# Two dense layers and a mixture of experts on one core: one gather for two pairs of experts, 21 weight slots, and activations placed at the weights' address modulo 256

## The chip, the core and the metric

The kernel runs on one core of a Trainium2 chip. The metric is the device time of one execution in microseconds (us), the median of several runs. The core's engines work side by side, each through its own queue in order: PE (TensorE, matrix products; PEld is its loading of the stationary operand, which the profile lists apart), DVE (VectorE), ACT (ScalarE), POOL (GpSimd) and SP (SyncE, which issues nearly all DMA transfers here). [...] The matrices come from HBM by DMA.

## The reference

The input is 256 rows of 1024 numbers in fp32. Two ordinary layers (a mixer, a gated feed-forward part and a gated per-layer embedding each) are followed by a convolution block, and that by a mixture of 32 experts, of which each row takes two:

```python
def hier_moe(h, w_rg, b_rg, w_re, b_re, w_gate, w_up, w_down):
    ...
    gate = grp_p[:, None] * jax.nn.softmax(top_val, axis=-1)
    expert = grp[:, None] * MOE_EXPERTS_PER_GROUP + top_idx
    ...
    def run_block(args):
        xb, e = args
        hid = jax.nn.silu(xb @ w_gate[e]) * (xb @ w_up[e])
        return hid @ w_down[e]
...
x = x + g1 * y
h = rmsnorm_2(x, norm_ffn_g[i]) * (1 + sc2) + sh2
x = x + g2 * hier_moe(h, ...)
return rmsnorm_2(x, final_g)
```

An expert has three matrices: gate and up of 1024 x 512, down of 512 x 1024, all fp32.

## The kernel before

**Dense part (0 to about 787 us).** Rows are two halves `h` of 128. Every fp32 product is made of three products of fp32r addends: an activation and a weight are each split into a high and a low addend, and `mm3` (L109) adds high x high, high x low and low x high in PSUM through `mm` (L101), the one place where these products are issued. The stationary operand is a block of 128 x 128 activations (`xTh`/`xTl`; in places `yTh`/`yTl`, `aTh`/`aTl`, `kvh`, `qlh`, `pTh` and their low parts), the moving one 512 columns of weights in a tile `hl` (high addends in its first half, low ones in its second; split by ACT and DVE in `prep`, L146). In the convolution's input product the roles are swapped for five of its eight parts: `hl` is stationary and `xTh`/`xTl` move, 256 columns.

**Where the operands lie.** A tile's address within its partition follows from the order and the sizes in which the pools hand them out. Of the built program, modulo 256 bytes: every `hl` starts at 224. `xTh`, `xTl` and the second layer's `aTh`, `aTl` start at 160; `yTh`, `yTl`, the first layer's `aTh`, `aTl`, and `kvh`, `qlh` with their low parts start at 128. Steps within these tiles are multiples of 512 bytes, so each product has one of these residues. Of products with 512 columns there are 2,112 with the stationary operand at 160 and 408 at 128; with 256 to 384 columns there are 276 more, and 240 with the roles swapped (stationary at 224, moving at 160).

**Experts (about 798 us to the end).** The 32 experts run as 16 pairs. For pair `i`:
- `pair_slots(i, False)` builds on DVE a table of 256 rows x 128 slots (64 per expert) that has a row's norm factor `rstd` where the row goes to the slot; `pair_slots(i, True)` the same with the gate's weight.
- `gather` (L1541) multiplies the rows `X` by this table on PE, in fp32: 2 PSUM banks, in each 4 blocks of 128 columns x 2 halves. ACT and DVE then bring the blocks to `xg`, in turn, with gain and shift. An fp32 product is two passes on PE, so a gather is 32 rows of the trace.
- `expert` (L1570): blocks `b` = 0, 1 (gate) and 2, 3 (up), each with one weight slot of each expert: 8 products of 64 x 512 that run side by side two by two.
- `down` (L1592): first `before(0)`, then the transposed hidden state, `before(1)`, and blocks 4 and 5 with the down matrices. The results, split in two addends, are added into the output by `combine2` during the next pair (L1633, L1634).

`back(j)` hangs the other work on these points: at j = 0 the combine for one half of the rows and the gather of pair i + 1, at j = 1 the other half and `way_back`. For pair 0 the gather stands in front of the expert (first bank) and after block 0 (second bank, `start`).

**Weights of the experts.** `preload` (L1106) has SP issue 192 transfers of 1 MB (numbered q; pair i uses q = 12 i to 12 i + 11, block b two of them) into 24 slots used in turn: 3 `early`, 2 `nexts`, 3 `ring`, 5 `wring`, 8 `split`, and 3 more: two tiles `w` and `spare`, which takes the place of `xTh` when the dense part has ended. A transfer into a slot waits for PE's last product with what is in it, and SP's queue is in order.

Of the kernel before, what the change touches and what calls it, by code (L numbers as in the profile page):

```python
# [8 lines left out]
F32 = mybir.dt.float32  # L9
# [19 lines left out]


@with_exitstack
def kernel(ctx, tc, A, out, stop=None):
# [4 lines left out]

    RING, SPLIT, EARLY, NEXT, WRING, MORE = SLOT_PLAN
    SLOTS = RING + SPLIT + EARLY + NEXT + WRING + MORE
    const = ctx.enter_context(tc.tile_pool(name="const", bufs=1))  # L40
# [530 lines left out]
    def ffn_ple(l, end, mid=None):  # L571
# [534 lines left out]
    def preload(n):  # L1106
        while len(moe_w) < min(n, 6 * NEXP):
# [3 lines left out]
            if s_ < EARLY:  # L1111
                t_ = early.tile([128, 2048], F32, name="ew", tag="ew")
            elif s_ < EARLY + NEXT:
                t_ = nexts.tile([128, 2048], F32, name="nw", tag="nw")
            elif s_ < EARLY + NEXT + RING:
                t_ = ring.tile([128, 2048], F32, name="raw", tag="raw")
            elif s_ < EARLY + NEXT + RING + WRING:
                t_ = wring.tile([128, 2048], F32, name="wr", tag="wr")
            elif s_ < SLOTS - MORE:
                t_ = split.tile([128, 2048], F32, name="hl", tag="hl")  # L1120
            else:
                t_ = spare if s_ == SLOTS - 1 else moe.tile([128, 2048], F32, name="w", tag="w", bufs=MORE - 1)
            pieces = 2 if q == 6 * NEXP - 1 else 1
# [361 lines left out]
    late = []  # L1485
    G1, G2, G3 = TG["rt"]
    for n in range(2):
        def ev_co(h, pt, n=n):
            t_ = small.tile([128, 512], F32, name="xf", tag="xf")
            tt(t_, pt, g1row[:, n * 512:(n + 1) * 512], MUL)  # L1490
            resid(h, n, t_)
            if n == 1 and h == 0:
                norm_stat(h)
                fill(G1, lambda: r_transpose(0, 0))
                fill(2, lambda: r_transpose(0, 1))
                fill(G2, lambda: r_logits(0))
                fill(G3, lambda: late.append(r_choose(0)))
# [34 lines left out]

    spare = xp.tile([128, 2048], F32, name="spare", tag="xTh")
    preload(SLOTS)

    yhl = xp.tile([128, 2, D], F32R, name="yhl", tag="xTl")
    yh, yl = yhl[:, 0, :], yhl[:, 1, :]
    xg = moe.tile([128, 8, 128], F32, name="xg")


    def gather(oh_r, n, gs=(0, 1)):  # L1541

        for g in gs:
            tp = pbank("w").rearrange("p (k t) -> p k t", k=4)
            for i in range(4):
                k = 4 * g + i
                for h in range(2):
                    T.matmul(tp[:, i, :n], X[:, h, k * 128:(k + 1) * 128], oh_r[:, h, :n], start=h == 0, stop=h == 1)  # L1548
            for i in range(4):
                k = 4 * g + i  # L1550
                if i % 2:
                    ts(xg[:, k, :n], tp[:, i, :n], moe_g[:, k:k + 1], modc[:, 24 + k:25 + k], MUL, ADD)
                else:
                    act(xg[:, k, :n], tp[:, i, :n], AF.Identity, scale=moe_g[:, k:k + 1], bias=modc[:, 24 + k:25 + k])
    def way_back(oh_g, n, exact=False, into=None):
# [13 lines left out]

    def expert(weights, n_e, between=None, after0=None):  # L1570

        n = 64 * n_e
        pg, pu = pbank("gu"), pbank("gu")
        for b in range(4):
            ws = weights(b)
            o = pg if b < 2 else pu
            for kk in range(4):
                for e in range(n_e):
                    k = 4 * (b % 2) + kk
                    T.matmul(o[64 * e:64 * e + 64, :], xg[:, k, 64 * e:64 * e + 64],  # L1580
                             ws[e][:, kk * 512:(kk + 1) * 512], start=k == 0, stop=k == 7)
# [56 lines left out]

    def pair_slots(i, back):
        t_ = moe.tile([128, 2, 128], F32, name="oh", tag="oh_g" if back else "oh_r", bufs=1)  # L1640
        for h in range(2):
            for e in range(2):
                q = 2 * i + e
                sc = gate[:, h, q:q + 1] if back else rstd[h][:, 0:1]
                ts(t_[:, h, 64 * e:64 * e + 64], iota64, rank[:, h, q:q + 1], sc, EQ, MUL)
        onehots[i, back] = t_

# [6 lines left out]
    def start_ends():  # L1654
# [3 lines left out]
        G.dma_start(rows_[0:1, D:2 * D], A["final_g"])  # L1658
        end.extend([rows_[:, 0:D], rows_[:, D:2 * D], R, early.tile([128, 2048], F32, name="ew", tag="ew")[:, 0:D]])

# [15 lines left out]

    prev = None
    pair_slots(0, False)
    gather(onehots[0, False], 128, (0,))

# [5 lines left out]
    def start():  # L1686
        gather(onehots[0, False], 128, (1,))
        for f in late:
            f()
        pair_slots(0, True)  # L1690
        ts(more, cnt, 64.0, None, ALU.is_gt)
# [4 lines left out]
        V.tensor_copy(nblk, upto[0:1, 31:32])  # L1696
        pair_slots(1, False)

    for i in range(NP):
# [7 lines left out]
        def back(j, i=i, prev=prev, final=final):  # L1707
            if prev is not None and j < 2:
                combine2(j, prev[0], i == 1, final)
                if final:  # L1710
                    gather_up(j)
            if not final and j == 0:
                gather(onehots[i + 1, False], 128)
            if j == 1:
                backs[i] = way_back(onehots[i, True], 128, not final)
            if i == NP - 2 and j == 5:
# [4 lines left out]
        if i:  # L1721
            pair_slots(i, True)
        if i and not final:
            pair_slots(i + 1, False)
        hid = expert(weights, 2, (lambda: spread(0)) if final else None, None if i else start)
        down(hid, weights, 2, end[3] if final else None, back, scaled=final, gates_of=lambda i=i: backs[i][1])
# [3 lines left out]
    bt = rtile("bt", 1, pool=moe)  # L1730
    V.memset(bt, 0.0)
    n_more = nc.values_load(nblk[0:1, 0:1], min_val=0, max_val=7)
    with tc.For_i(0, n_more, 1):
# [237 lines left out]
```

## Time and profile before

| what | us |
|---|---|
| median of 3 runs | 1268.66 (1268.04 to 1274.27) |
| the profiled execution | 1269.42 |
| its span in the trace | 1267.7 |
| PE busy in the span | 1212.2 (96%) |
| DVE, ACT, POOL busy | 670.8, 488.9, 76.3 |
| read from HBM | 358 MB |

A busy share is an average over stages that have different limits, and a busy PE is not one that does its work in the shortest time: the distance between the starts of two products that follow each other tells how long one of them holds PE. In the experts' part two things run side by side, PE through the pairs and the DMA through the 192 transfers; which of them sets the end is read from how far ahead of PE a transfer lands.

### The profile page before, as it was taken

To read this page: it belongs to the slowest core of one execution; us is meant where nothing else is said; L and a number is where in the kernel's file an instruction comes from. 1 tells how busy PE (TensorE), PEld (TensorE's weight loads), DVE (VectorE), ACT (ScalarE), POOL (GpSimd) and SP (SyncE) were. 2 spreads that over 40 slices of the span, in tenths; PEclk is the share of its full clock that TensorE was granted. 3 is DMA by queue.
4 is the path that set the end of the run, shared out by engine and by line. 5 is a ranking of instruction groups with operands and counts; after the bars stand their busy time and mean duration, and the time that the engine had idled before them with its cause. 6 is when DMAs were issued, how large, how long until landed. Compare 5 with 4: busy or idle time off the path is not lost. (4 is left out here: it accounts for less than half of the span.)

```text
span 1267.7 us, 16261 instructions
## 1 busy us (share of the span) xinstructions
PE 1212.2 (96%) x6320; PEld 840.9 (66%) x6323; DVE 670.8 (53%) x1188; ACT 488.9 (39%) x828; POOL 76.3 (6%) x105
## 2 busy tenths in 40 slices
PE   7999999999889999999998969899999999999996
PEld 5888888888777888888887937444444454444442
DVE  6767677577777687764465985422222222222214
ACT  7546544436785474444365513211111111111111
POOL 1101000001030000000003240000000000000000
PEclk9999999999999999999998989999999999999999
DMA  9644777774542189765553868999999999999970
GB/s 330 234 166 183 265 278 266 278 298 139 184 161 100 66 329 367 277 227 186 200 182 122 264 230 332 351 396 421 419 421 420 421 420 420 420 421 420 421 324 34
DMA packets 59950, 361.18 MB, mean 285 GB/s; under 512 B 7200, under 2 KB 10432, under 8 KB 21600
## 3 DMA queue, kind: packets, MB, share of 16 engines
q1 hardware_dynamic: 58752, 357.21, 73.2%
q0 software_dynamic: 976, 2.92, 0.7%
q8 instruction: 50, 0.82, 0.3%
q14 instruction: 28, 0.23, 0.1%
q10 hardware_dynamic: 144, 0.00, 0.0%
HBM read 358.15 MB, written 1.96 MB: 284 GB/s over the span
## 5 line engine op out<-in xcount | busy, mean ns | idle before, releaser
L102 PE MATMUL mm<-hl,xTh 128*128 128x512 f32 (+3 forms) x1376 | 423.4, 387 | 11.8 <-ACT hl L57 6.4
L61 DVE TENSOR_TENSOR hl<-raw,hl 128x1024 fp32r<-128x1024 f32 (+3 forms) x240 | 283.1, 1209 | 94.1 <-ACT hl L57 91.6
L102 PEld LDWEIGHTS mm<-hl,xTh 128*128 128x128 f32 x1376 | 256.3, 191 | 63.3 <-ACT hl L57 6.8
L57 ACT ACTIVATE hl<-raw 128x1024 fp32r<-128x1024 f32 (+3 forms) x240 | 240.9, 1033 | 142.5 <-PE mm L102 106.3
L102 PE MATMUL mm<-hl,xTl 128*128 128x512 f32 (+3 forms) x688 | 266.6, 388 | 2.5 <-DVE xTl L61 2.5
L102 PEld LDWEIGHTS mm<-hl,xTl 128*128 128x128 f32 x688 | 131.2, 191 | 27.0 <-DVE xTl L61 3.2
L1580 PE MATMUL gu<-hl,xg 128*64 128x512 f32 x448 | 111.4, 592 | 0.0
L102 PE MATMUL mm<-hl,aTh 128*128 128x512 f32 x352 | 110.2, 393 | 0.0
L61 DVE TENSOR_TENSOR hid<-gu,hid 128x512 f32<-128x512 f32 x16 | 11.1, 692 | 162.3 <-PE gu L1580 162.3
L57 ACT ACTIVATE xg<-w,modc,moe_g 128x128 f32<-128x128 f32 x64 | 29.3, 457 | 162.4 <-PE w L1548 147.1
L102 PEld LDWEIGHTS mm<-hl,aTh 128*128 128x128 f32 x352 | 66.1, 188 | 15.0
L1580 PEld LDWEIGHTS gu<-hl,xg 128*64 128x64 f32 x448 | 41.3, 137 | 49.9 <-issue 48.4
L70 DVE SCALAR_TENSOR_TENSOR yhl<-w,gc,yhl 128x512 fp32r<-128x512 f32 x30 | 22.5, 750 | 96.7 <-ACT yhl L57 94.8
L102 PE MATMUL mm<-hl,aTl 128*128 128x512 f32 x176 | 69.8, 397 | 0.0
L66 DVE TENSOR_SCALAR xg<-w,moe_g,modc 128x128 f32<-128x128 f32 x64 | 26.2, 410 | 69.4 <-ACT xg L57 69.4
L1548 PEld LDWEIGHTS w<-oh,X 128*128 128x128 f32 x512 | 59.6, 192 | 3.5 <-issue 1.6
L71 DVE SCALAR_TENSOR_TENSOR ada<-ada,crow 128x1024 f32<-128x1024 f32 x48 | 58.4, 1219 | 6.3 <-DMA ada<-in_ada_dram 6.3
L57 ACT ACTIVATE yhl<-w,gc 128x512 fp32r<-128x512 f32 x30 | 20.7, 689 | 106.1 <-PE w L1609 106.1
L1548 PE MATMUL w<-oh,X 128*128 128x128 f32 x512 | 60.3, 276 | 0.1
L1609 PE MATMUL w<-w,hid 128*64 128x512 f32 x128 | 59.3, 611 | 0.0
L1609 PE MATMUL w<-wr,hid 128*64 128x512 f32 x256 | 57.9, 598 | 0.0
L1580 PE MATMUL gu<-ew,xg 128*64 128x512 f32 x192 | 56.5, 593 | 1.2 <-ACT xg L57 1.2
(453 smaller groups left out, 1474.5 us busy)
## 6 DMA issues: line engine op xcount, KB each, us to landing
raw<-in_dense_dram SPq DMA_DIRECT2D x108, 1024.0 KB, 5.3
hl<-in_moe_dram SPq DMA_DIRECT2D x64, 1024.0 KB, 19.8
wr<-in_moe_dram SPq DMA_DIRECT2D x40, 1024.0 KB, 17.3
ada<-in_ada_dram SPq DMA_DIRECT2D x48, 512.0 KB, 7.5
ew<-in_moe_dram SPq DMA_DIRECT2D x24, 1024.0 KB, 17.8
raw<-in_moe_dram SPq DMA_DIRECT2D x24, 1024.0 KB, 19.8
nw<-in_moe_dram SPq DMA_DIRECT2D x16, 1024.0 KB, 19.2
w<-in_moe_dram SPq DMA_DIRECT2D x16, 1024.0 KB, 18.8
```

The costliest lines, as they stand in the source:

```text
L57: return S.activation(o, i, f, bias=bias, scale=scale)
L61: return (e or V).tensor_tensor(o, a, b, op=op)
L66: return (e or V).tensor_scalar(o, a, s1, s2, op0=op0, op1=op1)
L70: return V.scalar_tensor_tensor(o, a, s, b, op0=op0, op1=op1)
L71: return V.scalar_tensor_tensor(o, a, s, b, op0=op0, op1=op1, accum_out=accum_out)
L102: T.matmul(o, lhsT, rhs, start=start, stop=stop_)
L1548: T.matmul(tp[:, i, :n], X[:, h, k * 128:(k + 1) * 128], oh_r[:, h, :n], start=h == 0, stop=h == 1)
L1580: T.matmul(o[64 * e:64 * e + 64, :], xg[:, k, 64 * e:64 * e + 64], ws[e][:, kk * 512:(kk + 1) * 512], start=k == 0, stop=k == 7)
L1609: T.matmul(py[c][64 * e:64 * e + 64, :], hT[:, k, 64 * e:64 * e + 64], ws[e][:, kk * 1024 + c * 512:kk * 1024 + (c + 1) * 512], start=k == ...
```

## The change

1. **One gather for two pairs.** The normed rows X x rstd are kept as two fp32r addends in `xTh`/`xTl` (free by then): `xn_hi` on ACT, `xn_lo` on DVE. `two_pairs(i)` builds one table of 256 rows x 256 slots of zeros and ones for pairs i and i + 1, and `gather2` multiplies both addends by it: 4 groups of 2 blocks, in each 8 products of 256 columns, with one PSUM bank a group and an eviction of 128 x 256 per block. It runs in front of pair 0 (groups 0, 1 before block 0, groups 2, 3 after it) and at j = 0 of every odd pair; pairs 0, 2, 4, ... have no gather behind their up blocks. `expert` reads its half of the wider `xg`.
2. **21 slots.** The two tiles `w` and `spare` are gone: `xTh` and `xTl` stay in use to the end, and `yhl` and `xg` take the other room.
3. **Addresses.** Empty tiles (`shift_by`) of 64 bytes in front of `xTh` and of 32 bytes in front of `yTh`, of the first layer's `aTh`, and in `mixer1` move what follows. In the program built from the changed kernel all the activation addends of the dense part start at 224 modulo 256, as `hl` does. The order of the dense part's instructions is the same.

```diff
+def shift_by(pool, n):
+    gaps.append(n)
+    pool.tile([128, n // 4], F32, name=f"gap{len(gaps)}", tag=f"gap{len(gaps)}")
...
     X = xp.tile([128, 2, D], F32, name="X")
+    shift_by(xp, 64)
     xTh = xp.tile([128, 2, 8, 128], F32R, name="xTh", tag="xTh")
...
+    shift_by(l0, 32)
     wsT = l0.tile([128, 8, 128], F32, name="wsT")
...
+        if l == 0:
+            shift_by(ap_, 32)
         aTh = ap_.tile([128, 2, 22, 128], F32R, name="aTh")
...
+        shift_by(mp, 32)
         gmh = mp.tile([128, 512], F32, name="gmh")
...
+    xn = [t_.rearrange("p h k t -> p h (k t)") for t_ in (xTh, xTl)]
+    def xn_hi(h):
+        for c in range(2):
+            sl = slice(512 * c, 512 * c + 512)
+            act(xn[0][:, h, sl], X[:, h, sl], AF.Copy, scale=rstd[h][:, 0:1])
+    def xn_lo(h, c):
+        sl = slice(512 * c, 512 * c + 512)
+        stt(xn[1][:, h, sl], X[:, h, sl], rstd[h][:, 0:1], xn[0][:, h, sl].bitcast(F32), MUL, SUB)
...
             if n == 1 and h == 0:
                 norm_stat(h)
+                xn_hi(0)
+                for c in range(2):
+                    xn_lo(0, c)
...
     norm_stat(1, e=G)
+    xn_hi(1)
     r_logits(1)
...
+    def gather2(oh, gs):
+        for g in gs:
+            tp = pbank("w").rearrange("p (k t) -> p k t", k=2)
+            for i in range(2):
+                k = 2 * g + i
+                for h in range(2):
+                    for j in range(2):
+                        T.matmul(tp[:, i, :], xn[j][:, h, k * 128:(k + 1) * 128], oh[:, h, :],
+                                 start=j + h == 0, stop=j + h == 2)
+            for i in range(2):
+                gather_out(2 * g + i, tp[:, i, :], 256)
...
-    pair_slots(0, False)
-    gather(onehots[0, False], 128, (0,))
+    ones2 = [two_pairs(0)]
+    xn_lo(1, 0)
+    gather2(ones2[0], (0, 1))
+    xn_lo(1, 1)
...
-            if not final and j == 0:
-                gather(onehots[i + 1, False], 128)
+            if i % 2 and not final and j == 0:
+                gather2(ones2[0], (0, 1, 2, 3))
...
-SLOT_PLAN = 3, 8, 3, 2, 5, 3
+SLOT_PLAN = 3, 8, 3, 2, 5
```

Three places show it in the order of the instructions. On PE, at the end of pair 0 (`gu` is an expert's gate or up bank, `raw` and `wr` weight slots, L1597 the transposes of the hidden state, L1559 `way_back`, L1609 blocks 4 and 5), before:

```order
L1580 MATMUL gu<-raw,xg 64x512 x9
L1548 MATMUL w<-oh,X 128x128 x16
L1597 MATMUL w<-ident,hid 128x128 x4
L1559 MATMUL w<-ident,oh 128x128 x2
L1609 MATMUL w<-wr,hid 64x512 x16
```

and changed:

```order
L1624 MATMUL gu<-raw,xg 64x512 x9
L1641 MATMUL w<-ident,hid 128x128 x4
L1603 MATMUL w<-ident,oh 128x128 x2
L1653 MATMUL w<-wr,hid 64x512 x16
L1624 MATMUL gu<-wr,xg 64x512
```

The gather of pair 1 is no longer there; in pair 1 there stand 32 products of 256 columns in the place of the 16 of L1548.

On SP, the experts' weights around the end of the dense part (`hl` are the 8 slots of `split`), before:

```order
L1126 DMA wr<-in_moe_dram 128x2048 x5
L1126 DMA hl<-in_moe_dram 128x2048 x8
L1126 DMA w<-in_moe_dram 128x2048 x2
L1126 DMA spare<-in_moe_dram 128x2048
L1126 DMA ew<-in_moe_dram 128x2048 x3
```

and changed:

```order
L1138 DMA raw<-in_moe_dram 128x2048 x3
L1138 DMA wr<-in_moe_dram 128x2048 x5
L1138 DMA hl<-in_moe_dram 128x2048 x8
L1138 DMA ew<-in_moe_dram 128x2048 x3
L1138 DMA nw<-in_moe_dram 128x2048 x2
```

The first transfer that has to wait for an expert's product is now number 21, no longer number 24.

On DVE, between the ranks of the rows within their experts and the first evictions to `xg`, before:

```order
L70 SCALAR_TENSOR_TENSOR rank<-asg,aux 128x64
L66 TENSOR_SCALAR oh<-iota_5380,rank,rs 128x64 x4
L66 TENSOR_SCALAR xg<-w,moe_g,modc 128x128 x4
L65 TENSOR_SCALAR gs_6785<-keep_6587 128x1 x2
L70 SCALAR_TENSOR_TENSOR gs_6785<-gs_6785 128x1
```

and changed:

```order
L79 SCALAR_TENSOR_TENSOR rank<-asg,aux 128x64
L70 TENSOR_TENSOR oh_6742<-iota_5384,rank 128x256 x2
L79 SCALAR_TENSOR_TENSOR xTl<-X,rs,xTh 128x512
L75 TENSOR_SCALAR xg<-w,moe_g,modc 128x256 x2
L79 SCALAR_TENSOR_TENSOR xTl<-X,rs,xTh 128x512
L75 TENSOR_SCALAR xg<-w,moe_g,modc 128x256 x2
```

Two wider instructions build the table in place of four, and the low addend of the second half of the rows stands between them and the evictions.

## Rows read from the trace of the kernel before

**Rows 1.** Page, 40 slices of 31.7 us: PE's busy tenths, GB/s moved by DMA.

```profile
PE   7999999999889999999998969899999999999996
GB/s 330 234 166 183 265 278 266 278 298 139 184 161 100 66 329 367 277 227 186 200 182 122 264 230 332 351 396 421 419 421 420 421 420 420 420 421 420 421 324 34
```

**Rows 2.** Windows: length, busy us of PE, PEld, DVE, ACT, POOL; PEclk, DMA share, GB/s.

```profile
100.00:200.00 100.00, 100.00 (x455) 82.45 (x454) 70.77 (x122) 50.49 (x66) 0.57 (x1) 1.00 0.71 255
900.00:950.00 50.00, 49.24 (x258) 24.91 (x256) 12.74 (x34) 8.05 (x16) 0.00 (x0) 1.00 1.01 421
```

**Rows 3.** SP's timeline (start, length, what, count), two turns of the slots apart.

```profile
1066.41 17.74 SPq L1126 DMA_DIRECT2D hl<-in_moe_dram  x8
...
1186.20 17.73 SPq L1126 DMA_DIRECT2D hl<-in_moe_dram  x8
```

**Rows 4.** Timeline of PE, one pair's combine, gather, transposes, next pair's combine.

```profile
956.62 0.49 PE L1633 MATMUL acc<-yhl,ogT 128*128 128x512 f32 x1
...
957.65 3.73 PE L1548 MATMUL w<-oh,X 128*128 128x128 f32 x32
...
961.53 0.66 PE L1597 MATMUL w<-ident,hid 128*128 128x128 f32 x4
...
984.62 0.50 PE L1633 MATMUL acc<-yhl,ogT 128*128 128x512 f32 x1
```

**Rows 5.** Timeline and windows where the slots run out; issue-to-landing of these transfers.

```profile
793.80 0.42 SPq L1126 DMA_DIRECT2D spare<-in_moe_dram  x1
...
804.50 6.51 SPq L1126 DMA_DIRECT2D ew<-in_moe_dram  x3
...
804.00:806.00 2.00, 2.00 (x18) 1.60 (x15) 0.00 (x0) 0.00 (x0) 0.00 (x0) 1.00 0.49 70
...
DMA to landing us min/median/max: 4.7/6.9/11.3
```

**Rows 6.** Window in which the last weights land; PE's timeline in the last pair.

```profile
1225.00:1230.00 5.00, 5.00 (x25) 1.88 (x22) 0.50 (x3) 0.01 (x1) 0.00 (x0) 1.00 0.76 311
...
1231.73 7.09 PE L1580 MATMUL gu<-hl,xg 128*64 128x512 f32 x32
...
1245.37 1.11 PE L1609 MATMUL w<-hl,hid 128*64 128x512 f32 x1 [2.80 <-DVE ogT L1567]
...
1250.47 0.64 PE L1609 MATMUL w<-spare,hid 128*64 128x512 f32 x1
```

**Rows 7.** Timeline of PE: first and last low-addend product of four unbroken stretches.

```profile
245.96 0.40 PE L102 MATMUL mm<-hl,aTl 128*128 128x512 f32 x1
...
280.26 0.40 PE L102 MATMUL mm<-hl,aTl 128*128 128x512 f32 x1
...
580.26 0.39 PE L102 MATMUL mm<-hl,aTl 128*128 128x512 f32 x1
...
617.34 0.39 PE L102 MATMUL mm<-hl,aTl 128*128 128x512 f32 x1
...
690.34 0.28 PE L102 MATMUL mm<-hl,xTl 128*128 128x256 f32 x1
...
692.46 0.28 PE L102 MATMUL mm<-hl,xTl 128*128 128x256 f32 x1
...
697.19 0.28 PE L102 MATMUL mm<-xTl,hl 128*128 128x256 f32 x1
...
703.99 0.28 PE L102 MATMUL mm<-xTl,hl 128*128 128x256 f32 x1
```

**Rows 8.** Timeline: table and first block of the first pair; ACT and DVE on 128x256.

```profile
797.35 0.98 DVE L66 TENSOR_SCALAR oh<-iota,rank,rs 128x64 f32<-128x64 f32 x4
...
800.82 3.65 PE L1580 MATMUL gu<-ew,xg 128*64 128x512 f32 x16 [0.61 <-ACT xg L57]
...
761.14 0.60 ACT L57 ACTIVATE yc<-yc,vc 128x256 f32<-128x256 f32 x1 [3.98 <-DVE yc L61]
...
762.68 0.41 DVE L61 TENSOR_TENSOR xTl<-yc,xTh 128x256 fp32r<-128x256 f32 x1
```

More of the change, by code (lines that the diff above doesn't have):

```diff
@@ L28, in row_bcast @@
     return bass.AP(tensor=ap.tensor, offset=ap.offset, ap=[[0, parts], [1, n]])
+gaps = []
+def shift_by(pool, n):
+    gaps.append(n)
+    pool.tile([128, n // 4], F32, name=f"gap{len(gaps)}", tag=f"gap{len(gaps)}")
 @with_exitstack
@@ L36 @@
     ctx.enter_context(tc.manual_schedule())
-    RING, SPLIT, EARLY, NEXT, WRING, MORE = SLOT_PLAN
-    SLOTS = RING + SPLIT + EARLY + NEXT + WRING + MORE
+    RING, SPLIT, EARLY, NEXT, WRING = SLOT_PLAN
+    SLOTS = RING + SPLIT + EARLY + NEXT + WRING
     const = ctx.enter_context(tc.tile_pool(name="const", bufs=1))
@@ L1118, in preload @@
                 t_ = wring.tile([128, 2048], F32, name="wr", tag="wr")
-            elif s_ < SLOTS - MORE:
+            else:
                 t_ = split.tile([128, 2048], F32, name="hl", tag="hl")
-            else:
-                t_ = spare if s_ == SLOTS - 1 else moe.tile([128, 2048], F32, name="w", tag="w", bufs=MORE - 1)
             pieces = 2 if q == 6 * NEXP - 1 else 1
@@ L1531, in pbank, with gather_out, gather @@
         return psm.tile([128, 512], F32, name=tag, tag=tag, bufs={"acc": 4, "gu": 2, "w": 2}[tag])
-    spare = xp.tile([128, 2048], F32, name="spare", tag="xTh")
     preload(SLOTS)
-    yhl = xp.tile([128, 2, D], F32R, name="yhl", tag="xTl")
+    yhl = moe.tile([128, 2, D], F32R, name="yhl")
     yh, yl = yhl[:, 0, :], yhl[:, 1, :]
-    xg = moe.tile([128, 8, 128], F32, name="xg")
-    def gather(oh_r, n, gs=(0, 1)):
-        for g in gs:
+    xg = moe.tile([128, 8, 256], F32, name="xg")
+    def gather_out(k, src, n):
+        o = xg[:, k, :n]
+        if k % 2:
+            ts(o, src, moe_g[:, k:k + 1], modc[:, 24 + k:25 + k], MUL, ADD)
+        else:
+            act(o, src, AF.Identity, scale=moe_g[:, k:k + 1], bias=modc[:, 24 + k:25 + k])
+    def gather(oh, n):
+        for g in range(2):
             tp = pbank("w").rearrange("p (k t) -> p k t", k=4)
@@ L1547, in gather @@
                 for h in range(2):
-                    T.matmul(tp[:, i, :n], X[:, h, k * 128:(k + 1) * 128], oh_r[:, h, :n], start=h == 0, stop=h == 1)
+                    T.matmul(tp[:, i, :n], X[:, h, k * 128:(k + 1) * 128], oh[:, h, :n], start=h == 0, stop=h == 1)
             for i in range(4):
[L1550 to L1554, printed above, removed]
+                gather_out(4 * g + i, tp[:, i, :n], n)
+    def gather2(oh, gs):
[9 more added lines that the diff above has]
+                gather_out(2 * g + i, tp[:, i, :], 256)
     def way_back(oh_g, n, exact=False, into=None):
@@ L1568, in way_back, with expert @@
         return og_
-    def expert(weights, n_e, between=None, after0=None):
+    def expert(weights, n_e, between=None, after0=None, s0=0):
         n = 64 * n_e
@@ L1579, in expert @@
                     k = 4 * (b % 2) + kk
-                    T.matmul(o[64 * e:64 * e + 64, :], xg[:, k, 64 * e:64 * e + 64],
+                    T.matmul(o[64 * e:64 * e + 64, :], xg[:, k, s0 + 64 * e:s0 + 64 * e + 64],
                              ws[e][:, kk * 512:(kk + 1) * 512], start=k == 0, stop=k == 7)
@@ L1637, with pair_slots @@
     onehots, backs = {}, {}
-    def pair_slots(i, back):
-        t_ = moe.tile([128, 2, 128], F32, name="oh", tag="oh_g" if back else "oh_r", bufs=1)
+    def pair_slots(i):
+        t_ = moe.tile([128, 2, 128], F32, name="oh", tag="oh_g", bufs=1)
         for h in range(2):
@@ L1643, in pair_slots, with two_pairs @@
                 q = 2 * i + e
-                sc = gate[:, h, q:q + 1] if back else rstd[h][:, 0:1]
-                ts(t_[:, h, 64 * e:64 * e + 64], iota64, rank[:, h, q:q + 1], sc, EQ, MUL)
-        onehots[i, back] = t_
+                ts(t_[:, h, 64 * e:64 * e + 64], iota64, rank[:, h, q:q + 1], gate[:, h, q:q + 1], EQ, MUL)
+        onehots[i] = t_
+    def two_pairs(i):
+        t_ = moe.tile([128, 2, 256], F32R, name="oh2", tag="oh2", bufs=1)
+        for h in range(2):
+            tt(t_[:, h, :].rearrange("p (q s) -> p q s", q=4), iota64[:, None, :].to_broadcast([128, 4, 64]),
+               rank[:, h, 2 * i:2 * i + 4, None].to_broadcast([128, 4, 64]), EQ)
+        return t_
     zo = moe.tile([1, 2], BF16, name="zo")
@@ L1658, in start_ends @@
         G.dma_start(rows_[0:1, D:2 * D], A["final_g"])
-        end.extend([rows_[:, 0:D], rows_[:, D:2 * D], R, early.tile([128, 2048], F32, name="ew", tag="ew")[:, 0:D]])
+        end.extend([rows_[:, 0:D], rows_[:, D:2 * D], R, ring.tile([128, 2048], F32, name="raw", tag="raw")[:, 0:D]])
     def spread(j, on_dve=()):
@@ L1686, in start @@
     def start():
-        gather(onehots[0, False], 128, (1,))
+        gather2(ones2[0], (2, 3))
         for f in late:
             f()
-        pair_slots(0, True)
+        pair_slots(0)
         ts(more, cnt, 64.0, None, ALU.is_gt)
@@ L1696, in start @@
         V.tensor_copy(nblk, upto[0:1, 31:32])
-        pair_slots(1, False)
     for i in range(NP):
@@ L1721 @@
         if i:
[L1722 to L1725, printed above, removed]
+            pair_slots(i)
+        if i % 2 and not final:
+            ones2[0] = two_pairs(i + 1)
+        hid = expert(weights, 2, (lambda: spread(0)) if final else None, None if i else start, 128 * (i % 2))
         down(hid, weights, 2, end[3] if final else None, back, scaled=final, gates_of=lambda i=i: backs[i][1])
@@ L1731 @@
     V.memset(bt, 0.0)
+    spare = nexts.tile([128, 2048], F32, name="nw", tag="nw")
     n_more = nc.values_load(nblk[0:1, 0:1], min_val=0, max_val=7)
@@ L1753 @@
         e_reg = nc.values_load(eid[0:1, 0:1], engines=(mybir.EngineType.SP,), min_val=0, max_val=NEXP - 1)
-        oh_r = moe.tile([128, 2, 128], F32, name="oh", tag="oh_r", bufs=1)
+        oh_r = spare[:, D + 288:D + 544].rearrange("p (h t) -> p h t", h=2)
         oh_g = moe.tile([128, 2, 128], F32, name="oh", tag="oh_g", bufs=1)
```

2 lines of the change are left out of this document (1 added, 1 removed).

## The prediction

> **What bounds the kernel now.** I read the page's slices first [rows 1]: PE is busy nine tenths or more in nearly every slice, and the DMA moves 420 GB/s in a row of slices from about 850 us to 1200 us and far less before. So there are two regimes. The windows [rows 2] show them. [...] From 900 to 950 us PE is busy for 49.24 of 50 us and the DMA share is 1.01: both are full, and the window can't say which sets the end.
>
> The end says it. The slots come round every 24 transfers, and SP's rows for the same slots, two turns apart, start at 1066.41 and 1186.20 [rows 3]: 119.79 us for 48 transfers, 2.50 us each, so 29.95 us for a pair's twelve. PE takes 984.62 - 956.62 = 28.00 us for a pair [rows 4]. PE is the faster of the two, but it starts 24 transfers behind. The last weights land where the 311 GB/s of the window end, at 1225 + 5 x 311/420 = 1228.7, and PE comes to the last slot at 1250.47 [rows 6], 21.8 us later. So in the experts' part PE sets the end today, with 21.8 us to the DMA behind it. A saving on PE counts up to about there, and then the DMA takes over.
>
> **The gather.** Today a pair's gather is 32 passes in 3.73 us, and the transposes start at 961.53, 0.15 us after it [rows 4]. Without it they start once the hidden state is there, right after the combine: an even pair saves about 3.9 us. In an odd pair 32 products of 256 columns stand instead. Rows of such fp32r products have 2.12 us for 6 triples, 118 ns each, or 6.80 us for 20 triples, 113 ns each [rows 7], so 3.7 us of PE. But four groups share two banks, and two evictions (0.60 on ACT and 0.41 on DVE for 128x256 [rows 8], near 1.1 us with the hand-over) empty one: 0.94 us for the first group and four times 1.1 are 5.3 us until the last is out. The transposes want the bank of the third group, so the odd pair's loss is some 0.4 us (bounds -0.4 and +1.5). Two pairs save 3.5 us, 16 pairs about 28 us. PE's mean of 26.3 us a pair is then far below the DMA's 29.95, and the 21.8 us of margin are used up.
>
> **The slots.** Now the DMA sets the end, and three slots fewer make it start worse. At present the last transfer ahead of the experts is issued at 793.80; number 24 waits for block 0 and is issued at 804.50, and between 804 and 806 the DMA moves only 70 GB/s [rows 5]. It has run dry and has 168 transfers to go. In the changed kernel 171 are to go from there: 3 x 2.50 = 7.5 us more. An issue's data follow after 4.7 - 2.5 = 2.2 us of overhead [rows 5], of which 1.2 lie ahead of the data and 1.0 behind. From the issue at 804.1 (below): 805.3 + 171 x 2.50 = 1232.8, and one more gap of 1.0 us while blocks 0 and 1 free their slots slowly. The present kernel has 3.3 us of such gaps; with no gather in pair 0, blocks 4 and 5 come 3.4 us sooner and free what the later one waited for. The last data arrive at 1233.8, 5.1 us later than now.
>
> What follows them: the up block 3 of the last pair needs transfers 186 and 187, which land 4 x 2.50 - 1.0 = 9.0 us before the last data. It starts at 1235.2 today (half of the 32 rows from 1231.73) and the span ends 32.5 us later; blocks 4 and 5, behind the transposes and the 2.80 us wait for DVE [rows 6], have their weights by then. So the span would end at 1233.8 - 9.0 + 32.5 = 1257.3, against 1267.7: **10.4 us less**. With 24 slots it would be 18: the slots cost about 7.5 of it.
>
> **The start.** The table takes two instructions of about 0.41 in place of four in 0.98 us, the low addend some 0.7 us on DVE behind it, and only the fourth product waits for that. Then the first group needs 0.9 us and its first eviction 0.6. Block 0 starts at 800.82 today [rows 8]; I get 800.4, with bounds -1 and +1 us, and each us of it moves the end one for one. The high addends are on ACT while it waits for DVE's routing, and the low addends of the first half on DVE in a wait for PE: nothing, or 0.7 us if routing came behind them.
>
> **The addresses.** The sum's largest term has no row that shows it directly, since no fp32r product of the trace has both operands at one residue. Rows 7 show that the residue counts. Stationary at 128: 34.30 us for 49 triples, 233.3 ns a product. At 160: 37.08 us for 54 triples, 228.7 ns. [...] With 256 columns, stationary at 160 gives 117.8 ns, and swapped (224 stationary, 160 moving) 113.3. There are two readings. If the loss falls with the address as from 128 to 160, 4.6 ns for 32 bytes, 224 gains 9.2 ns over 160. If the 4.5 ns of the swapped rows is a cost per product, it gains 4.5. I take the middle, 6.8 ns, as an estimate: 2,112 x 6.8 = 14.4 us; the 408 at 128 gain 11.4 each, 4.7 us; the 276 shorter ones 4.5 each, 1.2 us. The 240 swapped ones lose the distance they have now or keep it: 0 (to 1.1). That is 20.3 us. Not all of it counts: slices with 8 or fewer tenths [rows 1] hold waits of PE for chains on other engines, where a shorter product only lengthens the wait. I take nine tenths, **18 us**. [...] DVE is at 0.71 in the dense window [rows 2] and the DMA too, so both can follow a PE that is 3% faster.
>
> [...]
>
> **The sum.** 1269.4 (the profiled execution; its span is 1267.7) - 10.4 - 18 = 1241.0; the median lies 0.8 lower than this execution, so 1240.
>
> **Rivals.**
> 1. The addresses do nothing: only the experts' part gains. 1268.7 - 10.4 = 1258. For it: the swapped rows differ in more than the address (moving in two runs of 128). Against it: 128 and 160 differ in the same stage with the same instructions.
> [...]
> [...]
> [...]
>
> **Chances.** The forecast with 1228 to 1252: 46%. Rival 1, 1252 to 1263: 27%. Rival 2, below 1228: 14%. Rival 3: 6%. Rival 4: 7%, inside the forecast's range or a little over. The range from 1222 to 1260 leaves out half of rival 2, rival 3 and the upper quarter of rival 1, just under 20%. Over 0.5% (6 us, about what a measurement can tell from no change) faster is everything but rival 3 and the top of rival 1: 0.88; within it 0.06; slower 0.06.
>
> **What would show it.** Right: the starts of dense triples are 0.66 to 0.67 us apart (0.687 and 0.700 now); the DMA idles for 8 to 11 us before the second turn of the slots and then runs at 420 GB/s to the end; PE waits for DMA in the later pairs; the span ends 23 to 25 us after the last weights. [...]

## The result, and the profile after

The changed kernel takes 1255.48 us (median; 1252.61 to 1258.29) against 1268.35 us for the kernel before in the same comparison: a ratio of 0.989, with the interval 0.9857 to 0.9924. That is 12.9 us less where 28 were forecast. It is faster, and inside the range, but the gain is less than half of the forecast; rival 1 (1252 to 1263) is where the time fell.

The page of the changed kernel: PE's busy tenths and the DMA's GB/s in 40 slices of 31.4 us, to be held against [rows 1].

```profile
PE   7999999999889999999998979999999999898996
GB/s 333 234 171 184 262 288 264 282 301 145 188 142 113 46 329 374 282 239 196 201 162 146 262 210 326 260 421 420 419 420 420 419 420 420 420 420 421 420 419 97
```

The 420 GB/s start a slice earlier, right behind a slice with 260 (before, 351 and 396 lead up to them), and go on to the last slice but one. PE has tenths of 8 near the end, where it had nines throughout. The windows say the same in one row each (columns as in [rows 2]):

```profile
900.00:1000.00 100.00, 98.83 (x488) 46.44 (x485) 20.96 (x48) 14.70 (x24) 0.00 (x0) 1.00 1.01 420
1000.00:1100.00 100.00, 94.37 (x440) 40.40 (x440) 17.42 (x41) 11.94 (x19) 0.00 (x0) 1.00 1.01 420
1100.00:1200.00 100.00, 91.91 (x436) 41.60 (x434) 18.00 (x40) 12.82 (x21) 1.11 (x2) 1.00 1.01 420
```

The DMA is full in all three, and PE is idle for more and more of them. What PE waited for from 795 us on (us in all, times, the longest):

```profile
PE gu L1624 <- DMA hl<-in_moe_dram: 5.9, 5, 1.3
PE gu L1624 <- DMA wr<-in_moe_dram: 5.8, 5, 1.3
PE w L1653 <- DVE ogT L1611: 2.8, 1, 2.8
PE acc L1671 <- issue: 2.2, 1, 2.2
PE w L1594 <- DVE xg L75: 2.1, 7, 0.3
PE w L1641 <- DVE xg L75: 2.1, 7, 0.3
PE gu L1624 <- DMA raw<-in_moe_dram: 1.1, 2, 0.6
```

The waits for weights are new: the transfers now set the end of the experts' part, as forecast. The two rows with `xg` are the odd pairs' price of the shared PSUM banks (`tp` in `gather2`): products to `w` wait for evictions to `xg`, 0.6 us a pair.

**Where the 11.2 us of the two profiled executions (spans of 1267.7 and 1256.5 us) come from.** The first expert block starts at 796.04 us, against 800.82 before [rows 8]: 4.8 us from the dense part and the start, where 18.4 were forecast. From that block to the end it is 460.5 us, against 466.9: 6.4 us from the experts' part, where 10.0 were forecast.

The dense products, first and last low-addend product of the stretches of [rows 7], on PE's timeline (start, length):

```profile
243.57 0.39 PE L111 MATMUL mm<-hl,aTl 128*128 128x512 f32 x1
...
276.89 0.39 PE L111 MATMUL mm<-hl,aTl 128*128 128x512 f32 x1
...
576.61 0.40 PE L111 MATMUL mm<-hl,aTl 128*128 128x512 f32 x1
...
613.37 0.39 PE L111 MATMUL mm<-hl,aTl 128*128 128x512 f32 x1
...
693.00 0.28 PE L111 MATMUL mm<-xTl,hl 128*128 128x256 f32 x1
...
700.20 0.28 PE L111 MATMUL mm<-xTl,hl 128*128 128x256 f32 x1
```

A triple is the three products of one `mm3`. 49 triples in 33.32 us are 226.7 ns a product (233.3 before, stationary at 128), 54 triples in 36.76 us are 226.9 (228.9 before, at 160). With the roles swapped, 20 triples take 7.20 us, 120.0 ns, and before 113.3: these became slower. So 2,112 x 2.0 = 4.2 us and 408 x 6.6 = 2.7 us gained, 240 x 6.7 = 1.6 us lost, and some 0.4 us lost on the shorter ones (those of 256 columns went from 117.7 to 119.8 ns): 4.9 us. With the means over all undisturbed products of the two traces in place of these stretches (229.1, 233.4 and 227.3 ns) it is 4.3 us.

Where the transfers run dry and start again, and where they end (PE's and SP's timeline, then windows):

```profile
796.04 3.65 PE L1624 MATMUL gu<-ew,xg 128*64 128x512 f32 x16
...
799.72 5.99 SPq L1138 DMA_DIRECT2D ew<-in_moe_dram  x3
```

```profile
790.00:800.00 10.00, 9.09 (x52) 4.59 (x51) 5.37 (x17) 1.32 (x3) 0.00 (x0) 1.00 0.02 6
800.00:802.00 2.00, 2.00 (x18) 1.76 (x18) 0.53 (x1) 0.75 (x2) 0.00 (x0) 1.00 0.68 135
...
1225.00:1230.00 5.00, 4.36 (x20) 2.22 (x18) 4.15 (x7) 0.60 (x1) 0.00 (x0) 1.00 0.88 359
1230.00:1235.00 5.00, 2.82 (x10) 0.91 (x12) 2.09 (x4) 0.00 (x0) 0.00 (x0) 0.86 0.11 46
```

The 21 slots are full at 790 us and the DMA stands still for 10 us, until block 0 has freed its two slots at 799.7. Counted as in the forecast, as if all bytes came at 420 GB/s, the last data arrive at 1225 + 5 x (359 + 46)/420 = 1229.8, 433.8 us after the start of block 0; the forecast had 433.4. This step was right to half a microsecond. In fact the rate falls at the end (295, 254 and 193 GB/s in the three microseconds from 1228 on), and data come in until about 1231.

The last pair (PE's timeline, then windows):

```profile
1221.99 3.65 PE L1624 MATMUL gu<-hl,xg 128*64 128x512 f32 x14
...
1232.18 0.64 PE L1653 MATMUL w<-hl,hid 128*64 128x512 f32 x1 [2.82 <-DVE ogT L1611]
...
1243.34 5.40 PE L1671 MATMUL acc<-raw,ogT 128*128 128x512 f32 x8 [2.16 <-issue]
```

```profile
1230.00:1240.00 10.00, 7.82 (x28) 2.20 (x30) 2.09 (x4) 0.00 (x0) 0.00 (x0) 0.83 0.06 23
1240.00:1250.00 10.00, 7.84 (x17) 2.83 (x14) 4.32 (x8) 2.61 (x7) 0.87 (x2) 0.83 0.01 2
```

Block 3 of the last pair has its weights at 1221.99, 426.0 us after block 0 where 424.4 were forecast, and the span ends 34.5 us later where 32.5 were forecast. These two make up the 3.6 us missing in the experts' part.

### The profile page after: what moved, and what is told of

It reads as the page before. It is cut to its first block, busy times and chain, and to the rows that moved or that the text cites. A ratio compares the mean times of both kernels' runs of the same rounds, so it can differ in the third digit from the quotient of the medians.

```text
span 1256.5 us, 15660 instructions
## 1 busy us (share of the span) xinstructions
PE 1191.1 (95%) x6064; PEld 816.7 (65%) x6067; DVE 655.1 (52%) x1112; ACT 481.4 (38%) x800; POOL 76.0 (6%) x105
## 5 line engine op out<-in xcount | busy, mean ns | idle before, releaser
L1624 PE MATMUL gu<-hl,xg 128*64 128x512 f32 x392 | 100.9, 594 | 5.9 <-DMA hl<-in_moe_dram 5.9
L1624 PEld LDWEIGHTS gu<-hl,xg 128*64 128x64 f32 x392 | 35.0, 137 | 61.9 <-issue 50.2
L1624 PE MATMUL gu<-wr,xg 128*64 128x512 f32 x216 | 62.3, 595 | 5.8 <-DMA wr<-in_moe_dram 5.8
L1653 PE MATMUL w<-hl,hid 128*64 128x512 f32 x184 | 48.9, 605 | 2.8 <-DVE ogT L1611 2.8
L66 ACT ACTIVATE xg<-w,modc,moe_g 128x256 f32<-128x256 f32 x32 | 18.1, 565 | 85.4 <-PE w L1594 85.4
L66 ACT ACTIVATE hid<-gu 128x512 f32<-128x512 f32 x16 | 9.6, 597 | 102.0 <-PE gu L1624 102.0
L1624 PE MATMUL gu<-raw,xg 128*64 128x512 f32 x152 | 44.7, 594 | 1.1 <-DMA raw<-in_moe_dram 1.1
L1624 PEld LDWEIGHTS gu<-wr,xg 128*64 128x64 f32 x216 | 20.4, 137 | 38.3 <-issue 25.9
L1624 PE MATMUL gu<-ew,xg 128*64 128x512 f32 x152 | 43.7, 594 | 0.4 <-DMA ew<-in_moe_dram 0.4
```

Of the source, the lines that this page charges most:

```text
L66: return S.activation(o, i, f, bias=bias, scale=scale)
L1624: T.matmul(o[64 * e:64 * e + 64, :], xg[:, k, s0 + 64 * e:s0 + 64 * e + 64], ws[e][:, kk * 512:(kk + 1) * 512], start=k == 0, stop=k == 7)
L1653: T.matmul(py[c][64 * e:64 * e + 64, :], hT[:, k, 64 * e:64 * e + 64], ws[e][:, kk * 1024 + c * 512:kk * 1024 + (c + 1) * 512], start=k == ...
```

## Experiments

In the table, "block 0" is the start of the first expert block and "last weights" the landing of the last weight transfer, both from the profiled execution. A landing is the event that releases a waiting engine; in the kernel before it came 2.3 us after the time at which the forecast counts the last data in (1231.0 against 1228.7), and in the changed kernel 2.1 us after it (1231.9 against 1229.8). Each ratio is to the kernel before on the same chip, whose median was 1268 to 1272 us.

| kernel | median us | ratio (95%) | block 0 | last weights | span |
|---|---|---|---|---|---|
| before | 1268.35 | | 800.8 | 1231.0 | 1267.7 |
| changed | 1255.48 | 0.989 (0.9857 to 0.9924) | 796.0 | 1231.9 | 1256.5 |
| changed, again | 1255.94 | 0.9883 (0.9862 to 0.9904) | 795.3 | 1231.2 | 1255.7 |
| addr_only | 1263.25 | 0.994 (0.9921 to 0.9958) | 796.2 | 1226.7 | 1263.1 |
| no_addr | 1260.42 | 0.9914 (0.9893 to 0.9934) | 798.2 | 1233.4 | 1258.0 |
| dist_128 | 1264.21 | 0.9958 (0.994 to 0.9976) | 806.1 | 1239.0 | 1261.9 |
| slots_19 | 1260.47 | 0.9925 (0.9905 to 0.9946) | 796.4 | 1237.3 | 1259.7 |
| no_odd_gather | 1256.87 | 0.9893 (0.9867 to 0.9919) | 794.5 | 1230.2 | 1254.7 |
| before_256 | 1264.08 | 0.9954 (0.9935 to 0.9973) | 794.5 | 1219.2 | 1261.2 |
| all_256 | 1250.13 | 0.9832 (0.9809 to 0.9856) | 796.3 | 1225.5 | 1248.4 |
| tail_first | 1245.70 | 0.9823 (0.9805 to 0.9841) | 793.0 | 1222.1 | 1242.4 |
| map_a, map_b, pad_256 | 1266.65, 1259.49, 1254.28 (one time each) | | 808.8, 805.0, 795.6 | 1243.6, 1236.4, 1231.4 | 1264.8, 1257.8, 1252.6 |

### The addresses alone, and everything else alone

`addr_only` is the kernel before with the four gaps of the change's diff:

```diff
     X = xp.tile([128, 2, D], F32, name="X")
+    shift_by(xp, 64)
...
+    shift_by(l0, 32)
...
+        if l == 0:
+            shift_by(ap_, 32)
...
+        shift_by(mp, 32)
```

> The kernel before with the changed kernel's address gaps alone: old gather, 24 slots, and all activation addends of the dense part at 224 modulo 256. Theory A (the addresses give what the two traces show product by product: 2,112 products at 229.0 to 227.3 ns are 3.6 us, 408 at 233.3 to 227.3 are 2.4 us, 240 with swapped roles at 113.3 to 120 lose 1.6 us): the dense part is 4.4 us shorter, the experts' part is unchanged at 466.9 us from the first block to the end, 1264.0 us. Theory B (the dense part's gain in the changed kernel came from something else, such as the rewritten start of the experts): 1268 us, no change. Theory C (my prediction: 18 us): 1250 us.

Measured: 1263.25 us. The first block's row:

```profile
796.19 3.65 PE L1593 MATMUL gu<-ew,xg 128*64 128x512 f32 x16 [0.61 <-ACT xg L65]
```

It is 4.6 us earlier than before, and the experts' part behind it takes 466.9 us, as before. Theory A holds in the trace; the medians give 7.6 us with an interval of 5.3 to 10.0, somewhat more. My forecast of 18 is excluded by both.

`no_addr` is the changed kernel with the same four lines taken out.

> The changed kernel without its address gaps: residues as before, gather for two pairs, 21 slots. Theory A: it loses the 4.4 us of the addresses, and the experts' part keeps its 6.4 us: 1260 us, with 460 us from the first block to the end. Theory B (the gain does not come from the addresses): 1255.5 us, as the changed kernel. Theory C (the parts do not add, the dense part hides in the same waits): between 1262 and 1268 us.

Measured: 1260.42 us, and 1258.0 - 798.2 = 459.8 us from block 0 to the end. The experts' part keeps its gain without the addresses. Block 0 starts 2.6 us earlier than before, but 2.4 of these are there at the last dense products already, which are the same in both kernels: the executions in the traces differ by one to two us in the dense part through short falls of PE's granted clock. The changed kernel's own profile has one (0.50 from 344 to 346 us):

```profile
340.00:350.00 10.00, 9.30 (x42) 7.61 (x43) 6.79 (x21) 5.03 (x12) 0.00 (x0) 0.83 0.55 203
```

Between 340 and 360 us it loses 1.6 us against the kernel before. So a trace gives the address term no better than to 2 us; the products' rows give 4.3 to 4.9, the trace of `addr_only` 4.6, and the medians 4.5 to 7.6.

### What it is about the address

`map_a` and `map_b` make each weight tile 32 bytes longer, so that the eight tiles start at eight residues; the gaps of the activations give other stationary residues.

```diff
-        hl = split.tile([128, 2, 1024], F32R, name="hl", tag="hl")
+        hl = split.tile([128, 2056], F32R, name="hl", tag="hl")[:, :2048].rearrange("p (c n) -> p c n", c=2)
```

> The changed kernel with its eight weight tiles each 32 bytes longer, so that the moving operand starts at all eight residues modulo 256 in turn, against stationary operands at 224 (xTh, xTl), 192 (first aTh), 160 (second aTh) and 128 (yTh). The spacing of 512-column products is read for every pair of residues. Theory equal: equal residues are best, 227 ns at 224 with 224, and it grows with the distance to some 233 ns. Theory stationary: the spacing depends on the stationary residue alone, 227 ns for xTh at all eight moving residues, 229 ns for 160, 233 ns for 128. Theory moving: it depends on the moving residue, as the 256-column rows suggest (113.3 ns with moving at 160, 118 to 120 with moving at 224): 512 columns from a tile at 160 then take some 220 ns or less.

> As map_a, with the stationary operands at 0 (xTh, xTl), 32 (first aTh), 64 (second aTh) and 96 (yTh). Theory equal: the best moving residue differs from stage to stage and equals the stationary one, 227 ns. Theory stationary: one spacing per stage, the same for all eight weight tiles; 0 could be as good as 224 or as bad as 128 (233 ns). Theory moving: the same order of the eight weight tiles in all four stages. In all of them the total lies within 8 us of 1256 us.

Measured, from the starts of all 512-column products of `xTh`, `xTl`, `aTh` and `aTl` that follow each other (addresses from the built program; moving minus stationary, modulo 256; mean ns from one start to the next):

```
distance          0      32     64     96     128    160    192    224
map_a             230.4  232.8  230.8  233.8  232.9  233.7  232.8  232.8
map_b             230.8  232.4  230.9  233.8  233.6  233.7  232.3  232.8
one distance      227.2         229.1  233.4  232.6
for all products  changed       before before dist_128
```

Each mean of the first two rows is over some 240 to 300 products. Sorted by the stationary residue alone, the means lie within 1.1 ns of each other; sorted by the moving one alone, the best tiles are those at 224 and 32 in `map_a` and those at 64 and 0 in `map_b`, whose stationary operands are for the most part at 224 and at 0: in each, the distances 0 and 64. Sorted by their distance, the two kernels agree to 0.7 ns in every column. So theory "equal" holds in its first half: distance 0 is best. Its second half falls: the time doesn't grow with the distance, 64 is nearly as good, and all the others cost about the same. What I hadn't expected is that distance 0 takes 230 ns where tiles at other distances take their turn with it, and 227.2 where all are at 0.

`dist_128` moves every activation of the dense part by 128 bytes and leaves the weights where they are:

```diff
-    shift_by(xp, 64)
+    shift_by(xp, 192)
```

> The changed kernel with 192 bytes ahead of xTh in place of 64: every activation addend of the dense part at 96, the weights still at 224, so a distance of 128 modulo 256 (weight slots ew, nw, raw move to 96, wr to 0). Theory distance: 512-column products at 233 ns as at this distance in map_a and map_b, in place of 227.2; 2,520 of them are 14.6 us, most of it in the start of the experts: block 0 at some 809 us, and the end some 13 us later, 1269 us, less 1 us for wr's five slots at residue 0. Rival (what counts is that all operands of the dense part have one residue, not which distance): 1256 us.

Measured: 1264.21 us. The first stretch of the rows above, and block 0:

```profile
247.38 0.39 PE L111 MATMUL mm<-hl,aTl 128*128 128x512 f32 x1
...
281.67 0.40 PE L111 MATMUL mm<-hl,aTl 128*128 128x512 f32 x1
...
806.13 3.65 PE L1624 MATMUL gu<-ew,xg 128*64 128x512 f32 x16
```

49 triples take 34.29 us, 233.3 ns a product, and block 0 starts 10.1 us later than in the changed kernel. The distance theory is borne out, the rival (one residue for all, whichever) is not. The end is 8 to 9 us later, not 13: block 0 came 10 us later in place of 13, and the transfers, with `wr`'s five slots now at residue 0, gave 2 to 3 us back (below; the last weights land 7.1 to 7.8 us later).

`pad_256` makes the tiles 256 bytes longer in place of 32, so that the distance stays 0 for all.

> The changed kernel with each of the eight weight tiles 256 bytes longer: residue 224 for all, distance 0 as in the changed kernel, but the tiles lie 8,448 bytes apart in place of 8,192. Theory (only the distance modulo 256 counts, and the 230.6 ns that distance 0 took in map_a and map_b came from neighbours at other distances): 227.2 ns, as in the changed kernel, 1256 us. Rival (the tiles' distance of 8,192 bytes counts): 230 ns or more, 1261 us.

Measured: 227.3 ns in the mean, 1254.28 us. Whether the tiles lie 8,192 or 8,448 bytes apart makes no difference that is seen (227.2 ns in the changed kernel). That a tile at distance 0 takes 230 ns between tiles at other distances is shown; why, stays open.

### The slots, and what PE saves

`slots_19` takes two more slots away.

```diff
-SLOT_PLAN = 3, 8, 3, 2, 5
+SLOT_PLAN = 3, 8, 3, 2, 3
```

> The changed kernel with 19 slots in place of 21 (wring 3 in place of 5); addresses of the dense part and of the slots as they are. Theory (the transfers stop when the slots are full, start again when the first expert block has freed its two, and then set the end): two more transfers are left at the restart, 2 x 2.50 = 5.0 us more, 1261 us, last weights 5 us later. Rival (the number of slots costs nothing while PE has enough ahead): 1256 us.

Measured: 1260.47 us, 4.5 to 5.0 us more than the two medians of the changed kernel; the last weights land at 1237.3 in place of 1231.2 to 1231.9. A slot is worth 2.3 to 2.5 us here by the times. The three that the change gave up would be 7 us or a little more by that, an estimate: no run has the new gather with 24 slots.

`no_odd_gather` leaves out the seven later gathers:

```diff
-            if i % 2 and not final and j == 0:
-                gather2(ones2[0], (0, 1, 2, 3))
```

> The changed kernel without the gathers of pairs 2 to 15 (all later pairs multiply the rows gathered for the first two; that part of the computation is left out): PE saves 7 x 3.9 = 27 us of products, ACT and DVE their evictions. Theory (the transfers set the end of the changed kernel from the middle of the experts' part on): the time stays within 2 us of the changed kernel, 1254 to 1257 us, and PE's waits for weights grow by some 25 us. Rival (PE still sets the end): 1229 us.

Measured: 1256.87 us, the same time as the changed kernel. PE's windows and its waits for weights:

```profile
1000.00:1100.00 100.00, 84.39 (x362) 32.21 (x358) 12.86 (x31) 8.30 (x13) 0.00 (x0) 0.98 1.01 420
1100.00:1200.00 100.00, 85.66 (x374) 34.59 (x375) 13.65 (x32) 8.30 (x13) 1.11 (x2) 1.00 1.01 420
```

```profile
PE gu L1624 <- DMA hl<-in_moe_dram: 14.6, 13, 2.5
PE gu L1624 <- DMA raw<-in_moe_dram: 7.3, 6, 1.3
PE gu L1624 <- DMA wr<-in_moe_dram: 7.3, 6, 1.3
PE gu L1624 <- DMA ew<-in_moe_dram: 5.2, 5, 1.3
PE gu L1624 <- DMA nw<-in_moe_dram: 4.6, 4, 1.3
```

The waits are 39.0 us, against some 13.7 in the changed kernel. Of the 27 us of products saved 25 have turned into waits for weights, and the time stands still: PE no longer sets the end.

### Where the slots lie

The maps showed something else. In the experts' part a transfer into a slot at residue 0 modulo 256 landed 2.42 to 2.45 us after the one ahead of it, into any other slot 2.47 to 2.50 us (means over transfers 70 to 184, for each tile of `hl` 5 or 6 of them, without the one gap of about 4 us in each trace):

```
map_a  hl at 0: 2.432   hl at 32 ... 224: 2.482 2.493 2.472 2.485 2.478 2.490 2.489   ew nw raw at 224: 2.500 2.494 2.483
map_b  hl at 0: 2.420   hl at 32 ... 224: 2.485 2.489 2.482 2.481 2.479 2.487 2.491   ew nw raw at 0:   2.431 2.433 2.449
```

The same slots `ew`, `nw` and `raw` are slow at 224 and fast at 0. `all_256` puts all 21 there, and the activations with them:

```diff
-    shift_by(xp, 64)
+    shift_by(xp, 96)
...
+    shift_by(rgap, 224)
     split = ctx.enter_context(tc.tile_pool(name="split", bufs=SPLIT, side="right"))
...
+    shift_by(wgap, 96)
     wring = ctx.enter_context(tc.tile_pool(name="wring", bufs=WRING, reuse_waits="tile"))
```

> The changed kernel with all weight slots at a multiple of 256 bytes (gaps of 96 bytes ahead of xTh and of wring, 224 bytes ahead of the split pool, in place of the 64 bytes ahead of xTh); the dense operands are at residue 0 too, so their distance stays 0. In map_b the landings of transfers into slots at residue 0 followed each other after 2.43 to 2.47 us, in all other slots and runs after 2.48 to 2.53 us. Theory address: the transfer is faster wherever it is written to a multiple of 256; with all 21 slots there, 171 transfers after the restart take 171 x 0.05 = 8.5 us less, and since the DMA sets the end of the changed kernel, it ends some 8 to 9 us earlier, near 1247 us. Theory run: the faster landings belonged to that run or to the place in the order, not to the address: 1256 us, 2.50 us per transfer as before.

> The changed kernel as it is, to be compared with the others on one chip: 1255 to 1258 us, 2.50 us per transfer, the first expert block at 796 us.

Measured: 1250.13 against 1255.94 us, with intervals that don't touch. The DMA's rate in the experts' part:

```profile
900.00:1000.00 100.00, 98.84 (x488) 46.55 (x484) 20.85 (x48) 14.72 (x24) 0.00 (x0) 1.00 1.01 426
1000.00:1100.00 100.00, 95.69 (x454) 41.17 (x453) 17.54 (x42) 11.95 (x19) 0.00 (x0) 1.00 1.01 427
```

426 to 427 GB/s in place of 420, a transfer in 2.462 us in place of 2.501: 171 x 0.039 = 6.7 us, and the last weights land 5.7 to 6.4 us earlier. Expected were 8 to 9 us, with 0.05 us a transfer. What differs between the slots is the address that is written: `map_a` shows 2.1% more for residue 32 and 2.3% more for 224 than for 0. Why a slot at residue 0 takes less, no run shows.

`before_256` does the same to 19 of the 24 slots of the kernel before.

> The kernel before (old gather, 24 slots) with the dense operands at distance 0 and 19 of its 24 weight slots at multiples of 256 bytes (wring's five stay at 160). Theory: transfers into the 19 slots take 2.45 us, but in this kernel PE sets the end, with some 22 us to the last weights: no gain over addr_only, 1263 us, and the last weights land 6 to 8 us earlier than there. Rival (the transfers set the end in the kernel before as well): 1256 us.

Measured: 1264.08 us, as `addr_only`, though the last weights land at 1219.2 in place of 1226.7. Faster transfers bring nothing that the times show where PE sets the end: nearly the same edit is worth 6 us behind this change.

### The end

`tail_first` is `all_256` with one copy moved ahead in the last pair:

```diff
                 combine2(j, prev[0], i == 1, final)
-                if final:
-                    gather_up(j)
+                if final and j == 0:
+                    gather_up(0)
...
                 backs[i] = way_back(onehots[i], 128, not final)
+                if final:
+                    gather_up(1)
```

> all_256 with one change in the last pair: DVE copies the table (ogT) ahead of the second half of its eight additions into the output, in place of behind all eight. In the changed kernel and in all_256 PE waits 2.8 us for this copy in blocks 4 and 5 of the last pair, and in the profiled runs of both the granted clock is at 0.66 to 0.83 in parts of the 20 us behind it. Theory (the end is one chain: last weights, blocks 3 to 5, sums; the wait is on it, and the wait makes the clock fall): the wait is 0.4 to 0.5 us, 2.3 us less, and up to 3 us more where the clock stays at 1.00: 1245 to 1248 us. Rival (something else is as late behind it, the products that clear the output's banks or the additions): 1250 us, as all_256.

Measured: 1245.70 us. The wait and the windows behind it:

```profile
1219.82 0.64 PE L1657 MATMUL w<-hl,hid 128*64 128x512 f32 x1 [0.17 <-DVE ogT L1615]
...
1229.33 5.40 PE L1675 MATMUL acc<-raw,ogT 128*128 128x512 f32 x8 [2.16 <-issue]
```

```profile
1220.00:1225.00 5.00, 5.00 (x24) 1.51 (x24) 2.34 (x4) 0.00 (x0) 0.00 (x0) 1.00 0.15 60
1225.00:1230.00 5.00, 2.84 (x14) 0.86 (x9) 1.39 (x3) 0.00 (x0) 0.00 (x0) 1.00 0.01 3
```

The wait is 0.17 us in place of 2.8, and from the last weights to the end it is 20.3 us in place of 22.9 in `all_256`. The clock is at 1.00 in both windows here and falls later, behind the wait of 2.16 us (0.71 in the mean from 1230 to 1240 us). By the times the gain over `all_256` isn't certain, since the two ratios' intervals overlap and the two ran on different chips; the wait's end is seen in the trace. This version's median is the lowest of all here.

How much the clock takes at the end is seen from `pad_256`, whose code differs from the changed kernel's in the tiles' padding alone:

```profile
1231.64 0.64 PE L1653 MATMUL w<-hl,hid 128*64 128x512 f32 x1 [2.80 <-DVE ogT L1611]
...
1241.12 3.70 PE L1671 MATMUL acc<-raw,ogT 128*128 128x512 f32 x8 [2.13 <-issue]
```

```profile
1230.00:1240.00 10.00, 7.35 (x32) 2.13 (x32) 2.95 (x6) 0.00 (x0) 0.00 (x0) 1.00 0.03 11
1240.00:1250.00 10.00, 5.61 (x12) 2.10 (x12) 6.17 (x9) 3.49 (x9) 2.22 (x4) 1.00 0.18 64
```

The same wait, the clock at 1.00 behind it, and 1252.6 - 1231.4 = 21.2 us from the last weights to the end, against 24.6 in the changed kernel (24.5 when it was traced again), whose clock was at 0.83 in the mean of these windows. So the same instructions take 3.4 us more or less there, by whether the granted clock stays at 1.00 or falls for a while: in the changed kernel's trace it is 0.50 from 1234 to 1237 us and again from 1244 to 1247.

## Why the prediction was wrong

- **What bounds the kernel: right.** PE set the end before, by 21.8 us from the counted data or 19.5 from the last landing (1231.0, with PE in the last slot at 1250.5), and the DMA takes over. `no_odd_gather` and `before_256` show both sides: taking work from PE no longer helps after the change, and faster transfers didn't help ahead of it.
- **The gather: right.** Matched by their place in the program, PE's products are further ahead of the kernel before by 3.9 us with every two pairs (17.3 us at 923, 21.2 at 979, 25.1 at 1035 us); 3.5 were forecast. It gets no further ahead than 25.1 us: at 1060 us it is 22.2 and at the end 11.2, and the rest is given back in waits for weights.
- **The slots: right as far as it was measured.** Two more slots away cost 4.5 to 5.0 us in `slots_19`, by 2.50 us each it would be 5.0; the 7.5 us for the three that the change gave up is not measured by itself. The counted last data were right to 0.4 us.
- **What follows the last weights: mis-sized by 3.6 us.** "9.0 us before the last data" took 1.0 us from the data to the release of PE. The landings come 2.1 us after the time at which their data are counted in, so block 3 started 1.5 us late. The 32.5 us behind it had been read from one execution, and in this one they were 34.5. The clock was lower for longer. In the kernel before it was low in one of the windows behind the wait:

```profile
1245.00:1250.00 5.00, 4.63 (x15) 1.41 (x16) 0.31 (x1) 0.00 (x0) 0.00 (x0) 0.68 0.00 0
1250.00:1255.00 5.00, 4.12 (x19) 1.09 (x17) 1.39 (x3) 0.00 (x0) 0.00 (x0) 1.00 0.00 0
```

In the changed kernel the mean from 1230 to 1250 us is 0.83. That is rival 4, a granted clock below 1.00 in the last pairs, but in the last pair alone, where part of it was in the 32.5 us already, and it cost some 2 us more (34.5 in place of 32.5). In `pad_256`, where the clock stayed at 1.00, the same stretch takes 31.1 us.
- **The addresses: the step that failed.** "I take the middle, 6.8 ns": the stretches show 2.0 (228.9 to 226.9). Both readings that I put the middle between are wrong. The loss doesn't fall evenly with the address: at 32 bytes' distance it is larger than at 64, and 160 against 224 was the second-best of all places already. And the 4.5 ns of the swapped rows was no price of the operands' being apart, since at distance 0 these rows take 120.0 ns, not 113.3 (and 119.8 with the roles not swapped); that stage lost 1.6 us, where "0 (to 1.1)" had been allowed. The gain for stationary 128 was mis-sized too: 6.6 ns, not 11.4. The sum is 4.9 us in place of 20.3, and rival 1 was nearly right in its time. No run shows the shorter products that rival 2 (below 1228) stands for: at distance 0 the stretches give 226.7 and 226.9 ns. One reading was off as well, without weight: 37.08 us for 54 triples are 228.9 ns, not 228.7, and the middle would have been 6.7 ns.
- **What it is in the address: shown in part.** The two operands' addresses act together: with the dense operands' distance changed from 0 to 128, the products take 5.4 ns more each (232.6 against 227.2), and the first expert block starts 10 us later. Which step of a product costs this time, no run shows.
- **The start: right.** 0.2 us by `no_addr` (2.6 less the 2.4 that the dense part was ahead already); 0.4 were forecast.

With the address term at 4.9 the sum would have been 1268.7 - 10.4 - 4.9 = 1253.4, and with the 3.6 us of the end 1257: 1255.48 was measured.

## What to carry to other kernels

An effect of which the trace shows two or three points has no slope yet: before a line is drawn through them and multiplied by thousands of products, one kernel that steps through all places (here eight tiles, each 32 bytes longer) gives the whole curve. Ask of every edit which engine sets the end in the kernel that it goes into: aligned slots were worth nothing that could be measured while PE was the bound and 6 us when the transfers were. And when a change makes the transfers the bound, look at how they are written and at the serial work behind the last of them next.

## What the runs showed of the hardware that was not expected

- The time of an fp32r product with 128 x 128 stationary and 512 moving columns depends on the distance of its two operands modulo 256 bytes: 227.2 ns at 0, 229.1 at 64, 232.6 to 233.4 at 96 and 128. Where tiles at different distances follow each other it is 230 to 234 ns, least at 0 and 64. With 256 columns the best was another distance (113.3 ns at 192, 117.7 at 64, 120.0 at 0), though the rows at 192 have the roles swapped and those at 64 don't; at 0 both are within 0.2 ns of each other.
- A 1 MB transfer into a tile that starts at a multiple of 256 bytes takes 2.42 to 2.47 us (2.462 on average where all slots lie so), into any other of the eight residues 2.47 to 2.51 us (2.501 on average where none lie so), when transfers follow each other without a gap.
- Of two kernels with the same instructions, apart from 256 bytes of padding, one kept the granted clock at 1.00 behind a wait of 2.8 us, and one had 0.83 in the mean of the 20 us around it, in both of its traced executions nearly the same time to the end (24.6 and 24.5 us, against 21.2). What decides between them stays open.
